# A third seven-product pair per gate and up unit, with two of its weight sums made by accumulating DMAs

## The chip, the cores and the metric

The kernel runs on one core of a Trainium2 chip. A time is the device time of one execution in microseconds (us). The kernel before takes 2226.62 us (median of 3 runs, 2225.67 to 2226.89). Profiles come from one execution of their own.

A core has engines that each work through their own list of instructions in order: TensorE (PE in the profile; PEld is its weight load) multiplies matrices into PSUM, eight banks of 512 floats per partition; VectorE (DVE), ScalarE (ACT) and GpSimd (POOL) work on elements; SyncE (SP) issues DMAs. An engine waits for another by semaphores, and what stands behind a waiting instruction in its list waits with it.

## The reference

One decoder layer in float32 on 256 tokens with 16 learned meta tokens ahead of them, model width 2048. Three blocks follow each other, each with a residual: a gated feed-forward, a mixer (differential attention and a short convolution, merged by gates), and a second gated feed-forward, then a last normalisation.

```python
def swiglu_ffn(h, w_gu, w_down):
    gate, up = jnp.split(h @ w_gu, 2, axis=-1)
    return (jax.nn.silu(gate) * up) @ w_down

h = rms_norm(s, norm_ffn2[layer])
s = s + 0.5 * swiglu_ffn(h, ffn2_w_gu[layer], ffn2_w_down[layer])
s = rms_norm(s, norm_final)
return s[:, N_META:]
```

The feed-forward width is 5632, so `w_gu` is 2048 x 11264: gate columns, then up columns. The change lies in the product with `w_gu` in the second feed-forward, where only the 256 real tokens are left.

## The kernel before

**Products in three matmuls.** Every float32 operand is split into a rounded high part and the remainder. For weights `parts` does it: ScalarE casts a tile into `wh`, VectorE subtracts it and writes `wl`. A product is then three matmuls: high by high, low by high, high by low. `wh` and `wl` have three buffers each (`W_BUFS`), so the splits run at most three tiles ahead of TensorE.

**The mixed unit.** In the second feed-forward the columns are taken in 11 groups of 512 gate and 512 up columns. Group 0 goes through a plain routine (`linear_tok`); the other ten each go through `gate_up_mix`, which calls `linear_mix`. Such a unit sums over 2048 input rows in 8 pairs of 128-row chunks. For one pair there are two token halves, two chunks and two column sets (gate and up), so a pair is a 2 x 2 by 2 x 2 block product. `KINDS` says for each of the 8 pairs how it is done:

- D (direct): eight block products. The weights come in two tiles of 1024 columns, each split and used in four products.
- S: a Strassen-like form with seven block products. It needs sums of the activation blocks, made once in `Mixed.pair` and kept in `sp`, and sums of the weight blocks, made anew in every unit. The weights come in four tiles: one of 512 columns (one product) and three of 1024 (two products each). The last two are sums and lie in `tt`: with w11, w12 the gate and up columns of the first chunk and w21, w22 those of the second, `tt` holds w11 + w12 (0), w12 + w22 (1), w11 + w12 + w22 (2) and that plus w21 (3). VectorE makes them by four additions (lines L507 to L510).

The products go to eight PSUM sums, "1" to "7" and "x"; `done` evicts each when its last product is in. The gating (L546 to L548: a sigmoid on ScalarE and two products on VectorE) follows from `flush`, called when the next unit's first pair has been used, and `back` transposes the gated result two tiles at a time for the down projection.

**Order of the work.** The program emits, for each tile, the split first and the tile's products two tiles later (`AHEAD` = 2, `step`). The framework's scheduler then fixes each engine's order when the kernel is built: by its own estimate of when things are ready it gives each engine the earliest emitted instruction that is ready, and gives buffers out as they come free. On the chip that order stands, and semaphores hold an instruction until its inputs are really there.

**Loads.** Weights come from memory through SP's queue into the buffers tagged `st`, 8 KB per partition each, of which there are four (`ST_BUFS`). In `linear_mix` a pair takes one buffer and two DMAs of 512 KB; an S pair takes a second buffer of the same tag for `tt`, without a DMA. A load stands in SP's queue until its buffer is free.

**Thirds.** The 11 groups go in three runs (4, 4 and 3 groups), each followed by two passes of the down projection (`linear_tok`, lines L318 to L320). So three of the ten mixed units come first after something else (group 1 after group 0, groups 4 and 8 after a down projection); the other seven follow another mixed unit. GpSimd's queue holds loads of small constants at the start and, in the last third, two loads of the last normalisation's gains (`gfin`).

Of the kernel before, what the change touches and what calls it, by code (L numbers as in the profile page):

```python
# [12 lines left out]
ALU = mybir.AluOpType  # L13
# [10 lines left out]
GW = GC * P  # L24
# [5 lines left out]
LAM_INIT = 0.8 - 0.6 * math.exp(-0.3 * 0)  # L30
KB = 2
W_BUFS = 3
ST_BUFS = 4
LB = 2
N_ACT = 24
EVICT_AT = 1
WARM = 6
HOLD = 3
LATER_AT = (4, 6)
KINDS = "DDDSDDDS"  # L40
AHEAD = 2


# [1 line left out]
def decoder_layer(ctx: ExitStack, tc: tile.TileContext, t, out):  # L45
    nc = tc.nc
# [7 lines left out]
    def bank(name):  # L54
        return psum.tile([P, 512], F32, tag="acc", name=name)
# [33 lines left out]
    def load_gain(g0, src):  # L89
# [5 lines left out]
        out=vrows[G_CONV:G_SUB, :], in_=t["conv_w"][0].rearrange("k (c p) -> (k c) p", p=P)  # L95
# [3 lines left out]
    for i, n in enumerate(("lambda_q1", "lambda_k1", "lambda_q2", "lambda_k2")):  # L99
# [7 lines left out]
        out=mask[:, T - P :],  # L107
        in_=mask[:, T - P :],
# [126 lines left out]
    def step(use):  # L235

        ahead.append(use)
        drain(AHEAD)
# [5 lines left out]
    def linear(act, chunks, w, k0, c0, t0, t1, name, evict, before=None, side_at=(5, 9, 13)):  # L244
# [7 lines left out]
        for b in range(0, len(chunks), kb):  # L252
# [5 lines left out]
            if b % nl == 0:  # L258
                st = wpool.tile([P, LB * kb, GW], F32, tag="st", bufs=ST_BUFS, name="st")
                ml = min(nl, len(chunks) - b)  # L260
# [40 lines left out]
    def flush():  # L301
        while pending:
            pending.pop(0)()

    def linear_tok(ops, chunks, k0, name, evict, side_at=(5, 9, 13), hold=0, after=None):
# [46 lines left out]
        for b, c in enumerate(chunks):  # L352
            if b % 2 == 0:
                st = wpool.tile([P, 2, 2, GW], F32, tag="st", bufs=ST_BUFS, name="st")
                r0 = (k0 + c) * P
# [9 lines left out]
    def parts(src, n=2):  # L365

        wh = wpool.tile([P, 2, GW], F32R, tag="wh", name="wh")[:, :n, :]
        wl = wpool.tile([P, 2, GW], F32R, tag="wl", name="wl")[:, :n, :]
        nc.scalar.copy(out=wh, in_=src)  # L369
        nc.vector.tensor_sub(wl, src, wh.bitcast(F32))  # L370
        return wh, wl
# [49 lines left out]
    class Mixed:  # L421
# [6 lines left out]
        def pair(self, p, f):  # L428
# [4 lines left out]
            nc.vector.tensor_sub(tl[:, :, 1, :], f, tl[:, :, 0, :].bitcast(F32))  # L433
            if KINDS[p] == "S":
                a11, a12, a21, a22 = (f[:, c, i * P : (i + 1) * P] for i in range(2) for c in range(2))
# [13 lines left out]
    def linear_mix(a, w, cols, name, done):  # L449

        nd, ns = KINDS.count("D"), KINDS.count("S")
        left = {k: 2 * nd * (k in "234x") + ns * (k != "x") for k in "1234567x"}
        ps = {}

        def product(k, left_op, wh, wl):
            first = k not in ps
            if first:
                ps[k] = bank(name + k)
            left[k] -= 1
            hi, lo = left_op
            nc.tensor.matmul(ps[k], hi, wh, start=first, stop=False)  # L467
            nc.tensor.matmul(ps[k], lo, wh, start=False, stop=False)  # L468
            nc.tensor.matmul(ps[k], hi, wl, start=False, stop=left[k] == 0)  # L469
            if left[k] == 0:  # L470
                done(k, ps[k])

        def use(p, n, products):

            for k, left_op, wh, wl in products:
                product(k, left_op, wh, wl)
            if p == len(KINDS) - 1 and n in (1, 2) and later:
                later.pop(0)()
            if n == (1 if KINDS[p] == "D" else 3):
                if p == 0:  # L480
                    flush()
                if side:
                    side.pop(0)()

        for p, kind in enumerate(KINDS):
            st = wpool.tile([P, 2, 2, GW], F32, tag="st", bufs=ST_BUFS, name="st")
            rows = w[2 * p * P : (2 * p + 2) * P, :].rearrange("(c p) f -> p c f", p=P)
            for q in range(2):
                nc.sync.dma_start(out=st[:, :, q, :], in_=rows[:, :, cols[q] : cols[q] + GW])
            (a11, a21), (a12, a22) = ([a.block(2 * p + c, i) for i in range(2)] for c in range(2))  # L490
            if kind == "D":
                tiles = [
                    (st[:, c], (("2", a1, 0), ("3", a1, 1), ("4", a2, 0), ("x", a2, 1)))
                    for c, (a1, a2) in enumerate(((a11, a21), (a12, a22)))
                ]
            else:
                s1, s2, s3, s4 = a.sums[p]
                tt = wpool.tile([P, 4, GW], F32, tag="st", bufs=ST_BUFS, name="tt")
                tiles = [
                    (st[:, 1, 1:2, :], (("3", s4, 0),)),  # L500
                    (st[:, :, 0, :], (("1", a11, 0), ("2", a12, 1))),
                    (tt[:, 2:4, :], (("6", s2, 0), ("4", a22, 1))),
                    (tt[:, 0:2, :], (("5", s1, 0), ("7", s3, 1))),
                ]
            for n, (src, products) in enumerate(tiles):
                if kind == "S" and n == 2:
                    nc.vector.tensor_add(tt[:, 0, :], st[:, 0, 0, :], st[:, 0, 1, :])  # L507
                    nc.vector.tensor_add(tt[:, 2, :], tt[:, 0, :], st[:, 1, 1, :])
                    nc.vector.tensor_add(tt[:, 3, :], tt[:, 2, :], st[:, 1, 0, :])
                    nc.vector.tensor_add(tt[:, 1, :], st[:, 0, 1, :], st[:, 1, 1, :])  # L510
                wh, wl = parts(src, src.shape[1])
                products = [(k, left_op, wh[:, j, :], wl[:, j, :]) for k, left_op, j in products]
                step(lambda p=p, n=n, products=products: use(p, n, products))

    def gate_up_mix(a, w_gu, g, m, gi):
# [3 lines left out]
        def done(k, ps):  # L519
# [21 lines left out]
            elif k == "7":  # L541
# [10 lines left out]
                pending.append(gated)  # L552

        linear_mix(a, w_gu, (g * GW, F + g * GW), "pg", done)

    def back(act, g, mt, k):
# [358 lines left out]
    for half in thirds:  # L915
# [10 lines left out]
        if final:  # L926
            for q in range(2):
                nc.gpsimd.dma_start(
                    out=gfin[q],
                    in_=t["norm_final"][q * W2 : (q + 1) * W2].rearrange("(o d) -> o d", o=1).to_broadcast([P, W2]),  # L930
# [47 lines left out]
```

## Time and profile before

| | |
|---|---|
| median of 3 runs | 2226.62 us |
| profiled execution, its own time | 2225.46 us |
| its span, first to last instruction | 2223.7 us |
| TensorE busy | 2205.9 us, 13608 matmuls |
| VectorE busy | 1376.3 us |
| ScalarE busy | 998.2 us |
| granted TensorE clock, mean | 0.998 |
| bytes moved by DMA | 401.95 MB, of it 1.21 MB on GpSimd's queue |

In the groups of a profile a row gives line, engine, operation, what is written and read, shapes and count; then busy time in us and the mean of one in ns; then the engine's idle time just before and what ended it. A row of the waits says which instruction waited for which, the total in us, how often, and the longest. A row of the order of time begins with the start from the span's begin and the length, both in us, and ends in brackets with the idle time before it. A matmul's length is longer than the distance to the next one, since matmuls overlap. "L507" is line 507 of the kernel before.

### The profile page before, as it was taken

To read this page: it belongs to the slowest core of one execution; us is meant where nothing else is said; L and a number is where in the kernel's file an instruction comes from. 1 tells how busy PE (TensorE), PEld (TensorE's weight loads), DVE (VectorE), ACT (ScalarE), POOL (GpSimd) and SP (SyncE) were. 2 spreads that over 40 slices of the span, in tenths; PEclk is the share of its full clock that TensorE was granted. 3 is DMA by queue.
4 is the path that set the end of the run, shared out by engine and by line. 5 is a ranking of instruction groups with operands and counts; after the bars stand their busy time and mean duration, and the time that the engine had idled before them with its cause. 6 is when DMAs were issued, how large, how long until landed. Compare 5 with 4: busy or idle time off the path is not lost.

```text
span 2223.7 us, 33100 instructions
## 1 busy us (share of the span) xinstructions
PE 2205.9 (99%) x13608; PEld 1989.5 (89%) x13608; DVE 1376.3 (62%) x1792; ACT 998.2 (45%) x1244; POOL 6.4 (0%) x17
## 2 busy tenths in 40 slices
PE   9999999999999999999999999999999999999998
PEld 8999999999999999898988888888888888888886
DVE  7555554455555565667765554668776578846875
ACT  6444343334434443444444444455454445534544
POOL 0000000000000000000000000000000000000000
PEclk9999999999999999999999999999999999999999
DMA  7555455555555455444555555555566555665563
GB/s 233 176 180 176 171 172 178 181 171 171 176 180 175 171 171 186 156 142 144 170 189 189 190 189 189 177 184 172 188 200 200 187 190 189 208 211 182 178 225 113
DMA packets 192023, 401.95 MB, mean 181 GB/s; under 512 B 8676, under 2 KB 8736, under 8 KB 191872
## 3 DMA queue, kind: packets, MB, share of 16 engines
q1 hardware_dynamic: 191232, 398.49, 53.0%
q8 instruction: 106, 1.74, 0.3%
q0 software_dynamic: 544, 1.21, 0.2%
q14 instruction: 45, 0.37, 0.0%
q10 hardware_dynamic: 96, 0.14, 0.0%
HBM read 397.71 MB, written 2.10 MB: 180 GB/s over the span
## 4 chain that ended last, share of the span: by engine, by line
PE 97%; DVE 1%; ACT 1%; DMA 0%; issue 0%; ACTq 0%; DVEq 0%
PE pg L467 5%; PE pg L469 5%; PE pg L468 5%; PE pg L282 4%; PE pg L280 4%; PE pd L282 4%; PE pu L282 4%; PE pu L280 4%; PE pg L281 4%; PE pd L280 4%; PE pd L281 4%; PE pu L281 4%; PE pd L320 4%; PE pd L318 4%; PE pd L319 4%; PE o L278 3%
## 5 line engine op out<-in xcount | busy, mean ns | idle before, releaser
L271 DVE TENSOR_TENSOR wl<-st,wh 128x1024 fp32r<-128x1024 f32 x392 | 478.5, 1223 | 442.4 <-ACT wh L270 442.1
L270 ACT CAST wh<-st 128x1024 fp32r<-128x1024 f32 x392 | 411.4, 1050 | 613.9 <-PE pd L281 146.9
L370 DVE TENSOR_TENSOR wl<-st,wh 128x1024 fp32r<-128x1024 f32 (+1 forms) x360 | 426.9, 1192 | 280.0 <-ACT wh L369 279.1
L369 ACT CAST wh<-st 128x1024 fp32r<-128x1024 f32 (+1 forms) x360 | 368.3, 1030 | 472.3 <-PE pgx L468 154.9
L280 PE MATMUL pg<-h,wh 128*128 128x272 f32 x704 | 203.3, 290 | 2.0 <-ACT wh L270 2.0
L280 PE MATMUL pu<-h,wh 128*128 128x272 f32 x704 | 203.3, 289 | 0.0
L282 PE MATMUL pu<-h,wl 128*128 128x272 f32 x704 | 203.0, 288 | 0.0
L282 PE MATMUL pd<-m,wl 128*128 128x272 f32 x704 | 203.0, 288 | 0.0
L280 PE MATMUL pd<-m,wh 128*128 128x272 f32 x704 | 202.9, 288 | 0.0
L281 PE MATMUL pd<-m,wh 128*128 128x272 f32 x704 | 202.4, 288 | 0.0
L281 PE MATMUL pu<-h,wh 128*128 128x272 f32 x704 | 202.4, 288 | 0.0
L281 PE MATMUL pg<-h,wh 128*128 128x272 f32 x704 | 202.4, 288 | 0.0
L282 PE MATMUL pg<-h,wl 128*128 128x272 f32 x704 | 201.1, 290 | 0.0
L467 PE MATMUL pg<-wh,hn 128*128 128x512 f32 x420 | 163.6, 390 | 0.0
L468 PE MATMUL pg<-wh,hn 128*128 128x512 f32 x420 | 163.5, 389 | 0.0
L469 PE MATMUL pg<-wl,hn 128*128 128x512 f32 x420 | 160.3, 391 | 0.0
L318 PE MATMUL pd<-wh,m 128*128 128x512 f32 x352 | 137.6, 391 | 0.0
L319 PE MATMUL pd<-wh,m 128*128 128x512 f32 x352 | 137.0, 389 | 0.0
L320 PE MATMUL pd<-wl,m 128*128 128x512 f32 x352 | 135.9, 390 | 0.0
L280 PEld LDWEIGHTS pg<-h,wh 128*128 128x128 f32 x704 | 132.9, 189 | 2.3 <-ACT wh L270 2.3
L281 PEld LDWEIGHTS pg<-h,wh 128*128 128x128 f32 x704 | 133.3, 189 | 0.0
L281 PEld LDWEIGHTS pu<-h,wh 128*128 128x128 f32 x704 | 132.7, 189 | 0.0
(279 smaller groups left out, 4536.4 us busy)
## 6 DMA issues: line engine op xcount, KB each, us to landing
st<-in_ffn_w_gu_dram SPq DMA_DIRECT2D x184, 512.0 KB, 4.3
st<-in_ffn_w_down_dram SPq DMA_DIRECT2D x88, 1024.0 KB, 5.1
st<-in_ffn_w_gu_dram SPq DMA_DIRECT2D x84, 1024.0 KB, 4.8
st<-in_w_in_dram SPq DMA_DIRECT2D x48, 1024.0 KB, 5.1
st<-in_w_gate_dram SPq DMA_DIRECT2D x64, 512.0 KB, 4.3
st<-in_w_branch_dram SPq DMA_DIRECT2D x32, 512.0 KB, 4.5
st<-in_w_out_dram SPq DMA_DIRECT2D x16, 1024.0 KB, 5.0
xin<-in_x_dram SPq DMA_DIRECT2D x8, 256.0 KB, 7.3
```

What stands on the lines that cost most here:

```text
L270: nc.scalar.copy(out=wh[:, :m, :], in_=sw)
L271: nc.vector.tensor_sub(wl[:, :m, :], sw, wh[:, :m, :].bitcast(F32))
L280: nc.tensor.matmul(a, wh[:, i, f], act.part(c, 0, t0, t1), start=first, stop=False)
L281: nc.tensor.matmul(a, wh[:, i, f], act.part(c, 1, t0, t1), start=False, stop=False)
L282: nc.tensor.matmul(a, wl[:, i, f], act.part(c, 0, t0, t1), start=False, stop=last)
L318: nc.tensor.matmul(ps, hi, wh[:, q, :], start=first, stop=False)
L319: nc.tensor.matmul(ps, lo, wh[:, q, :], start=False, stop=False)
L369: nc.scalar.copy(out=wh, in_=src)
L370: nc.vector.tensor_sub(wl, src, wh.bitcast(F32))
L467: nc.tensor.matmul(ps[k], hi, wh, start=first, stop=False)
L468: nc.tensor.matmul(ps[k], lo, wh, start=False, stop=False)
L469: nc.tensor.matmul(ps[k], hi, wl, start=False, stop=left[k] == 0)
```

## The change

`KINDS` becomes "DDSDDSDS": three S pairs (places 2, 5 and 7, counted from 0) where there were two (places 3 and 7). For an S pair, w12 is no longer loaded into `st`. Instead `tt`[0] is loaded with w11 and `tt`[1] with w22 by SP, and GpSimd's queue issues, for each, a DMA that adds w12 to what lies there. The additions L507 and L510 go; those that build `tt`[2] and `tt`[3] stay. A fifth buffer of the tag `st` comes in, and the memory set aside for GpSimd's DMA descriptors is set to 4096 bytes per partition.

```diff
-ST_BUFS = 4
+ST_BUFS = 5
...
-KINDS = "DDDSDDDS"
+KINDS = "DDSDDSDS"
...
             for q in range(2):
-                nc.sync.dma_start(out=st[:, :, q, :], in_=rows[:, :, cols[q] : cols[q] + GW])
+                c = q if kind == "S" else 0
+                nc.sync.dma_start(out=st[:, c:, q, :], in_=rows[:, c:, cols[q] : cols[q] + GW])
...
                 tt = wpool.tile([P, 4, GW], F32, tag="st", bufs=ST_BUFS, name="tt")
+                for q in range(2):
+                    nc.sync.dma_start(out=tt[:, q, :], in_=rows[:, q, cols[q] : cols[q] + GW])
+                    nc.gpsimd.dma_start(out=tt[:, q, :], in_=rows[:, 0, cols[1] : cols[1] + GW], accum_op=ALU.add)
...
                 if kind == "S" and n == 2:
-                    nc.vector.tensor_add(tt[:, 0, :], st[:, 0, 0, :], st[:, 0, 1, :])
                     nc.vector.tensor_add(tt[:, 2, :], tt[:, 0, :], st[:, 1, 1, :])
                     nc.vector.tensor_add(tt[:, 3, :], tt[:, 2, :], st[:, 1, 0, :])
-                    nc.vector.tensor_add(tt[:, 1, :], st[:, 0, 1, :], st[:, 1, 1, :])
...
-    nc = _bacc.Bacc("TRN2", target_bir_lowering=False, num_devices=1)
+    nc = _bacc.Bacc("TRN2", target_bir_lowering=False, num_devices=1, dynamic_dma_scratch_size=4096)
```

## The prediction

> **What bounds the kernel now.** I read the page first, then the groups of the second feed-forward (1500 us to the end), the waits, and the order of time on TensorE and VectorE around one seven-product pair.
>
> From the page:
>
> ```profile
> span 2223.7 us, 33100 instructions
> PE 2205.9 (99%) x13608; PEld 1989.5 (89%) x13608; DVE 1376.3 (62%) x1792; ACT 998.2 (45%) x1244; POOL 6.4 (0%) x17
> ...
> PE 97%; DVE 1%; ACT 1%; DMA 0%; issue 0%; ACTq 0%; DVEq 0%
> ```
>
> TensorE carries the chain; only fewer products, or fewer stalls of TensorE, can shorten it. The change touches only the ten mixed units, so their rows count. TensorE in the order of time, just where such a unit goes from the second to the third tile of its first S pair:
>
> ```profile
> 1857.62 0.39 PE L468 MATMUL pg<-wh,hn 128*128 128x512 f32 x1
> ...
> 1858.53 0.39 PE L469 MATMUL pg<-wl,hn 128*128 128x512 f32 x1
> 1859.34 0.50 PE L467 MATMUL pg<-wh,sp 128*128 128x512 f32 x1 [0.42 <-ACT wh L369]
> ```
>
> Two readings. The 0.39 us is a length; the pitch, over four of them (three left out), is (1858.53 - 1857.62) / 4 = 0.2275 us, and that is what a matmul costs. And here the pitch breaks: 1859.34 - 1858.53 = 0.81 us, a stall of 0.58 us. The waits tell how often, and what is late:
>
> ```profile
> PE pg L467 <- ACT wh L369: 2.1, 5, 0.4
> ...
> ACT wh L369 <- DVE tt L509: 21.3, 7, 3.2
> ...
> DVE tt L507 <- DMA st<-in_ffn_w_gu_dram: 6.2, 3, 2.8
> ```
>
> In 7 of 10 units the cast of the summed weights waits for the last sum (L509) on VectorE; in 5 of them TensorE stands still for it, in 2 it only just does not. The other 3 units, first after a down projection, show none of it. The third row is used below.
>
> **The change, part by part.**
>
> *Products.* One more S pair in place of a D pair: 7 products instead of 8, 3 matmuls each. 3 x 0.2275 = 0.68 us a unit, 10 units: -6.8 us. This lies on TensorE, on the path.
>
> *Where the first S pair stands.* It moves from place 3 to place 2, so TensorE comes to its third tile 24 x 0.2275 = 5.46 us sooner. VectorE before that point, in the unit above:
>
> ```profile
> 1847.64 1.22 DVE L370 TENSOR_TENSOR wl<-st,wh 128x1024 fp32r<-128x1024 f32 x1
> 1848.78 1.21 DVE L547 TENSOR_TENSOR cgate<-cgate,u2x 128x1024 f32<-128x1024 f32 x1
> 1849.91 1.22 DVE L370 TENSOR_TENSOR wl<-st,wh 128x1024 fp32r<-128x1024 f32 x1
> 1851.05 1.21 DVE L548 TENSOR_TENSOR cup<-cup,cgate 128x1024 f32<-128x1024 f32 x1
> 1852.18 1.81 DVE L370 TENSOR_TENSOR wl<-st,wh 128x1024 fp32r<-128x1024 f32 x2
> 1853.92 0.68 DVE L507 TENSOR_TENSOR tt<-st 128x512 f32<-128x512 f32 x1
> 1855.10 1.23 DVE L370 TENSOR_TENSOR wl<-st,wh 128x1024 fp32r<-128x1024 f32 x1 [0.49 <-ACT wh L369]
> 1856.24 0.68 DVE L508 TENSOR_TENSOR tt<-tt,st 128x512 f32<-128x512 f32 x1
> 1856.84 0.69 DVE L510 TENSOR_TENSOR tt<-st 128x512 f32<-128x512 f32 x1
> 1857.44 0.68 DVE L509 TENSOR_TENSOR tt<-tt,st 128x512 f32<-128x512 f32 x1
> ```
>
> VectorE works without a gap until 1854.60: it is still evicting the unit before (L547, L548) and splitting. The change takes two splits of the D pair at place 2 (1.13 us each from start to start) and L507 and L510 out of this stretch, 3.5 us against the 5.46 us that TensorE comes sooner. In this clock: L547 at 1848.78, the small split at 1849.91 (+0.60), L548 at 1850.51 (+1.13), the second split at 1851.64 (+1.14), the first remaining sum at 1852.78 (+0.72, since the next reads it; pitch below), the second at 1853.50, done 1854.18. TensorE starts 1859.34 - 1858.12 = 1.22 us after the last sum: 1855.40. It could at 1858.53 + 0.23 - 5.46 = 1853.30. Stall 2.1 us, where it was 0.58: +1.5 us, 5 units. The milder kind:
>
> ```profile
> 1804.94 1.21 DVE L547 TENSOR_TENSOR cgate<-cgate,u2x 128x1024 f32<-128x1024 f32 x1
> ...
> 1812.72 0.68 DVE L508 TENSOR_TENSOR tt<-tt,st 128x512 f32<-128x512 f32 x1
> 1813.44 0.69 DVE L509 TENSOR_TENSOR tt<-tt,st 128x512 f32<-128x512 f32 x1
> ...
> 1815.06 0.39 PE L469 MATMUL pg<-wl,hn 128*128 128x512 f32 x1
> 1815.35 0.50 PE L467 MATMUL pg<-wh,sp 128*128 128x512 f32 x1
> ```
>
> Same steps from 1804.94: TensorE at 1811.56, could at 1809.83: 1.7 us where it was 0.06, +1.65 us, 2 units. The first units of a third have room, a row from each side of it:
>
> ```profile
> 1769.21 1.23 DVE L370 TENSOR_TENSOR wl<-st,wh 128x1024 fp32r<-128x1024 f32 x1 [2.46 <-ACT wh L369]
> ```
>
> VectorE idles 2.46 us before one split there; 0 for 3 units. Sum: 5 x 1.5 + 2 x 1.65 = +10.8 us. Ends: 0 (the gating products fall behind the sums) and +15.
>
> *The two sums by DMA.* Each S pair now needs, before its sums: the slot of tt free, a 256 KB load on SP's queue, its landing, then an accumulating DMA of 256 KB on POOL's queue, which waits for that landing. No accumulating DMA is in the trace. Nearest rows:
>
> ```profile
> DMA to landing us min/median/max: 3.4/4.3/6.4
> ...
> st<-in_ffn_w_gu_dram SPq DMA_DIRECT2D x184, 512.0 KB, 4.3
> ...
> gfin<-in_norm_final_dram POOLq DMA_DIRECT2D x2, 512.0 KB, 8.4
> ...
> vrows<-in_norm_mix_dram POOLq DMA_DIRECT2D x1, 8.0 KB, 4.9
> ```
>
> The load: 3.4 us or a little less, being half as large. The accumulation: from 4.9 us (8 KB on POOL's queue) to twice 8.4 = 16.8 us; I take 8, near the row of 512 KB, since it reads 256 KB of weights and the 256 KB that it adds to. Chain: 11.4 us, bounds 8 to 20. SP's next loads stand behind the load's wait for the slot, the pair's second accumulation behind the first. [...]
>
> How long it may take: five buffers of that tag, 11 takings a unit. The tt at place 5 takes the slot of the st at place 2, free when the second sum there is done (1854.18). TensorE reaches the third tile at place 5 after 2 S tiles, two D pairs and 2 S tiles (69 matmuls), 15.7 us after 1855.40; less 1.22 and two sums, the accumulated tile may come at 1868.5: 14.3 us. The tt at place 7 takes the slot of the D pair at place 4: from that pair's second tile TensorE has 66 matmuls to go, 15.0 us, less the same 2.6: 12.4 us and the lead that the split had over TensorE. That at place 2 takes the slot of the st at place 7 of the unit before: 69 matmuls again, 13.1 us and that lead. So 11.4 us would do, if VectorE took the sums when they are needed. But its order is fixed when the kernel is built, by the scheduler's own estimate of landings, and that is too early already for one plain load:
>
> ```profile
> 1561.49 0.69 DVE L507 TENSOR_TENSOR tt<-st 128x512 f32<-128x512 f32 x1 [2.77 <-DMA st<-in_ffn_w_gu_dram]
> ```
>
> L507 stood at the head of VectorE's queue for 2.77 us until a load landed (6.2 us in 3 units), with the splits of later tiles behind it; TensorE had weights in hand and lost nothing. For a load and an accumulation in a row the error is more: 2.1 us (6.2 / 3) for the load, and up to 8.4 - 4.3 = 4.1 us if POOL's DMAs are planned like SP's; together 2 to 6 us. What waits behind the sums: splits, casts (their wh buffers), then TensorE. 2.8 us were free in a stretch of D tiles; at place 7 the wait falls among the tiles of place 5, where a tile lasts 0.68 to 1.37 us of TensorE and covers less. Per S pair at places 5 and 7: 0 to 3.4 us (6.2 - 2.8), I take 1.0: 20 pairs, +20 us, ends 0 and +68. At place 2 the VectorE backlog hides it, 0.
>
> *The rest.* VectorE per unit: two splits fewer, four more (one small), 8 sums become 6: 35.4 of 44.0 us busy as before.
>
> ```profile
> 1858.60:1902.60 44.00, 43.58 (x196) 35.47 (x194) 35.43 (x40) 22.29 (x26) 0.00 (x0) 1.00 0.56 192
> ```
>
> DMA share 0.56 at 8.4 MB a unit; 10.8 MB after (9.2 by SP, 1.6 by POOL), 12.3 with the second read: 0.72 to 0.82, not a bound, 0. POOL's 60 issues lie on an engine that is busy 6.4 us in all, and the only others in this stage, the two of gfin, are through before the last third's units begin: 0. The fifth buffer lets loads run earlier everywhere, but no row of TensorE waits for one: 0. The third set of activation sums (four small sums, a cast and a split, once) hides beside the first unit, where TensorE shows no wait: 0. The smaller descriptor scratch: 0.
>
> **Sum** against the profiled execution (span 2223.7, its own time 2225.46): -6.8 + 10.8 + 20 = +24 us, 2249.5; that execution stands 1.2 us below the median of 2226.62, so 2250 of the median.
>
> **The rivals.**
>
> 1. *The chain is in time and the sums stand late enough.* Only the backlog at place 2 is left: -6.8 + 10.8 = +4.0, 2230.6. For it: the 14.3 us against 11.4. Against it: the L507 row. This stands on the 0.2% line (4.5 us, about what a measurement of this kernel can tell from no change).
> 2. *Faster: neither wait is there.* The scheduler puts the gating behind the sums at place 2, and the chain is in time. With L548 alone behind (1.13 us) the stalls are 1.0 and 0.6, +3 us: 2222.8. With L547 too they are gone, and the old ones (5 x 0.58 + 2 x 0.06 = 3 us) with them: 2216.8. Middle 2219.8. It decides once VectorE has over 1 us less ahead of the sums. For it: VectorE is busy only 35.4 of 44.0 us. Against it: the gating stands earlier in the program than place 2.
> 3. *The accumulation is slow.* At 16.8 us the chain is 20.2, 5.9 us over the 14.3 of place 5 in ten units, 59, and as much as 41 more at place 7, of which the stall at place 5 covers a part: +4 and 60 to 100, 2290 to 2330.
>
> **How the numbers follow.** Forecast 0.45, rival 1 0.18, rival 2 0.20, rival 3 0.17. Faster by over 0.2%: rival 2, 0.20. Within: half of rival 1, 0.09. Slower: 0.71. Range: from the middle of rival 2, 2219, to 2292 (forecast with most of +68), which leaves out most of rival 3; the forecast's own range is 2231 to 2290.
>
> **What would show it.** Matmuls 13608 - 30 = 13578; POOL 60 more DMA rows. In the waits, VectorE's first sum waiting for a DMA of tt, some 20 to 30 times, and TensorE or ScalarE waiting for VectorE's splits after it. At place 2 the stall near 2 us in 7 units. The landing of the accumulation near 8 us; under 5 points to rivals 1 and 2, over 12 to rival 3. The prediction is wrong if the sums wait for no DMA, or if VectorE's order at place 2 has the sums ahead of the gating.

## The result and the profile after

The changed kernel takes 2318.51 us (median of 4 runs, 2314.31 to 2324.7) against 2226.57 us: a ratio of 1.0416, 95% interval 1.0392 to 1.0440. It is slower by 92 us, above the predicted 2250 and above the range.

The page of the profile after (profiled execution 2317.39 us):

```profile
span 2315.5 us, 33444 instructions
...
PE 2230.2 (96%) x13578; PEld 2001.4 (86%) x13578; DVE 1387.0 (60%) x1797; ACT 1015.0 (44%) x1265; POOL 58.4 (3%) x77
...
q0 software_dynamic: 9184, 16.94, 4.1%
...
PE 85%; DVE 6%; DMA 5%; issue 2%; ACT 1%; DVEq 0%; ACTq 0%; SPq 0%; POOLq 0%
```

The 30 matmuls are gone. But the chain that ended last, 97% TensorE before, now runs for 6% over VectorE and for 5% over DMA. The waits say which DMA (line numbers of the changed kernel: L502 issues the accumulating DMAs, L511 and L512 are the two sums):

```profile
DVE tt L511 <- DMA tt<-in_ffn_w_gu_dram: 92.8, 23, 8.1
...
PE pg L469 <- DVE wl L370: 57.6, 12, 7.6
...
ACT wh L369 <- DVE tt L512: 32.2, 7, 4.7
...
PE pg L467 <- ACT wh L369: 11.8, 7, 1.7
```

The first sum waits for an accumulation 23 times in 30, for 92.8 us. TensorE waits in two places: 57.6 us for the low parts of weights (L370), for which its waits before have no row, and 11.8 us for casts behind the sums (2.1 us before). The order of time shows how the first comes about. This is the end of one unit, from the last buffer's release on; SPq is SyncE's queue:

```profile
1663.40 1.19 SPq L501 DMA_DIRECT2D tt<-in_ffn_w_gu_dram  x2
...
1667.92 1.73 POOL L502 DMA_DIRECT2D tt<-in_ffn_w_gu_dram  x2 [11.06 <-DVE wl L370]
...
1668.26 2.00 ACT L369 CAST wh<-tt 128x1024 fp32r<-128x1024 f32 x2 [1.67 <-PE pgx L468]
...
1670.56 0.39 PE L468 MATMUL pg<-wh,sp 128*128 128x512 f32 x1
1675.97 0.69 DVE L511 TENSOR_TENSOR tt<-tt,st 128x512 f32<-128x512 f32 x1 [8.12 <-DMA tt<-in_ffn_w_gu_dram]
1676.70 0.69 DVE L512 TENSOR_TENSOR tt<-tt,st 128x512 f32<-128x512 f32 x1
1677.31 2.35 DVE L370 TENSOR_TENSOR wl<-tt,wh 128x1024 fp32r<-128x1024 f32 x2
1678.58 0.80 PE L469 MATMUL pg<-wl,sp 128*128 128x512 f32 x1 [7.64 <-DVE wl L370]
1679.18 0.63 PE L467 MATMUL pg<-wh,hn 128*128 128x512 f32 x1
1679.60 0.63 PE L468 MATMUL pg<-wh,hn 128*128 128x512 f32 x1
```

Read it from L511. This is the sum for place 7, and it reached the head of VectorE's queue at 1667.85 (1675.97 - 8.12), just as its accumulation was being issued. So VectorE stood for the whole flight. Behind L511 and L512 in the queue are the two splits of `tt` (L370), and these belong to place 5: ScalarE had cast those tiles from 1668.26 on. TensorE does the two matmuls that need only the high part, up to 1670.56, and then has nothing until 1678.58. The tile that L511 prepared was not wanted before all of place 5 and the D pair at place 6 were through.

There is a second loss. After the stall matmuls start every 0.42 us (1679.18, 1679.60), not 0.2275. The same stretch by engine, with the granted clock as the last column but two, and 490 us of the stage:

```profile
1678.50:1690.00 11.50, 11.42 (x38) 9.21 (x39) 5.44 (x6) 3.53 (x4) 0.00 (x0) 0.73 0.58 187
...
1500.00:1990.00 490.00, 440.70 (x1862) 355.74 (x1861) 322.75 (x373) 220.11 (x245) 36.37 (x42) 0.94 0.66 198
```

The same 490 us in the kernel before:

```profile
1500.00:1990.00 490.00, 488.31 (x2178) 400.83 (x2178) 356.94 (x412) 237.65 (x262) 0.91 (x2) 1.00 0.57 192
```

The granted clock was 0.73 there and 0.94 in the stage, where before it was 1.00. From 1490 us on the records show it at half for 82 us, in fifteen pieces of 3.4, 6.8 or 10.2 us, each beginning during a stall or within 1.7 us of its end. Two more pieces are not counted, 3.4 us at the start of the kernel and 8.4 us at its end, which the kernel before has too (3.4 and 8.1). The fifteen pieces begin whole multiples of 3.413 us apart. Stalls of 1.9 us were enough for one: all five of them here, and two of five in the run with late sums.

The account: over the matmuls from 1490 us to the end I added what each start-to-start distance has above the pitch. Before: about 7.5 us. After: about 106 us. The difference, 98 to 99 by the pitch that one takes, less the 6.8 us of products saved, is some 92, and the spans differ by 91.8. Of the 106, 57.7 us are ten stalls at place 7's sums, one a unit (2.3 to 7.8 us each), 13.0 us are seven stalls at place 2, 1.9 us lie at place 5, some 4 us are the small unevenness that was there before, and the rest, about 29 us, is matmuls at half clock. Three of the ten stalls at place 7 are short, 2.3 to 2.9 us: the accumulation there was issued 1.2 to 1.4 us before the sum came up, and landed 4.0 to 4.4 us after its issue, against 6.1 to 8.2 in the other seven. Why it landed sooner is open.

### The profile page after: what moved, and what is told of

Its sections match the earlier page's. It is cut to its first block, busy times and chain, and to the rows that moved or that the text cites. A ratio compares the mean times of both kernels' runs of the same rounds, so it can differ in the third digit from the quotient of the medians.

```text
span 2315.5 us, 33444 instructions
## 1 busy us (share of the span) xinstructions
PE 2230.2 (96%) x13578; PEld 2001.4 (86%) x13578; DVE 1387.0 (60%) x1797; ACT 1015.0 (44%) x1265; POOL 58.4 (3%) x77
## 3 DMA queue, kind: packets, MB, share of 16 engines
q0 software_dynamic: 9184, 16.94, 4.1%
## 4 chain that ended last, share of the span: by engine, by line
PE 85%; DVE 6%; DMA 5%; issue 2%; ACT 1%; DVEq 0%; ACTq 0%; SPq 0%; POOLq 0%
DMA tt<-in_ffn_w_gu_dram 5%; PE pg L282 4%; PE pg L280 4%; PE pd L282 4%; PE pu L282 4%; PE pu L280 4%; PE pd L280 4%; PE pg L281 4%; PE pd L281 4%; PE pu L281 4%; PE pd L320 3%; PE pd L318 3%; PE pd L319 3%; PE pg L469 3%; PE o L278 3%; PE g L320 3%
## 5 line engine op out<-in xcount | busy, mean ns | idle before, releaser
L370 DVE TENSOR_TENSOR wl<-st,wh 128x1024 fp32r<-128x1024 f32 (+1 forms) x360 | 422.4, 1178 | 277.9 <-ACT wh L369 276.9
L467 PE MATMUL pg<-wh,hn 128*128 128x512 f32 x390 | 156.2, 401 | 0.0
L468 PE MATMUL pg<-wh,hn 128*128 128x512 f32 x390 | 155.6, 399 | 0.0
L469 PE MATMUL pg<-wl,hn 128*128 128x512 f32 x390 | 152.5, 404 | 1.6 <-DVE wl L370 1.5
```

## The experiments

Two theories stood after this. **Place in the queue:** the accumulations are fast enough, but the scheduler put the place-7 sums ahead of place 5's splits, where everything behind them waits. **Landing:** the accumulations come too late whatever the order, so that TensorE waits for them anyway.

### The sums later in VectorE's queue

The two sums are held behind the split of the first tile of their own S pair (places 2, 5 and 7).

```diff
-                    nc.vector.tensor_add(tt[:, 2, :], tt[:, 0, :], st[:, 1, 1, :])
-                    nc.vector.tensor_add(tt[:, 3, :], tt[:, 2, :], st[:, 1, 0, :])
+                    with tc.issue_after(split_ins[-2]):
+                        nc.vector.tensor_add(tt[:, 2, :], tt[:, 0, :], st[:, 1, 1, :])
+                        nc.vector.tensor_add(tt[:, 3, :], tt[:, 2, :], st[:, 1, 0, :])
```

> The changed kernel with its two remaining sums held, in VectorE's order, behind the split of the first tile of their own S pair; nothing else differs. Theory Q (place in the queue): the loss is that the sums of place 7 stand in VectorE's order ahead of the splits of place 5's summed tiles and wait there, up to 8.1 us, for an accumulation that TensorE does not need until a pair and a half later. Then the stalls at place 7 (57.7 us in ten units) and the half-clock stretches after them go; left are the 6.8 us gained in products and about 10 us lost at place 2: 2228 to 2240 us. Rival L (late chain): the load and the accumulation in a row are simply too slow for their slot; then the stall only moves to the cast of the summed tile and the time stays over 2280 us.

Measured: 2233.51 us, ratio 1.0033 [1.0020, 1.0046]. 85 us of the 92 are back. Its waits (L471 is the low-part matmul, L514 and L515 the sums):

```profile
PE pg L469 <- ACT wh L371: 11.8, 7, 1.8
```

```profile
DVE tt L514 <- DMA tt<-in_ffn_w_gu_dram: 3.8, 4, 1.3
...
ACT wh L371 <- DVE tt L515: 32.2, 7, 4.7
```

The 57.6 us are gone entirely, and the sum waits for an accumulation 4 times instead of 23, 1.3 us at most. Bytes, transfers and buffers are the same, so the landing theory falls: taken where they are needed, the accumulations are there. What is left is the seven stalls at place 2, and VectorE's order in front of one shows why:

```profile
1636.01 1.22 DVE L553 TENSOR_TENSOR cup<-cup,cgate 128x1024 f32<-128x1024 f32 x1
1637.15 1.22 DVE L372 TENSOR_TENSOR wl<-st,wh 128x1024 fp32r<-128x1024 f32 x1
1638.29 0.68 DVE L514 TENSOR_TENSOR tt<-tt,st 128x512 f32<-128x512 f32 x1
1639.00 0.69 DVE L515 TENSOR_TENSOR tt<-tt,st 128x512 f32<-128x512 f32 x1
```

No gap, and the gating of the unit before (L553) just ahead. The stall behind it was 1.9 us, the predicted kind.

### Late at place 7 alone

As above, but held only where `p == 7`; at places 2 and 5 the sums are issued as in the changed kernel.

> The changed kernel with the two sums held behind the split of the S pair's first tile at place 7 alone; at places 2 and 5 they are issued as in the changed kernel. Theory (the loss is the place-7 sums standing ahead of the split of place 5's summed tiles: 57.7 us of TensorE's stalls, and the half clock after them): what is left is the 13.0 us of the seven stalls at place 2, the 1.9 us at place 5 and the half clock of some 7 us behind these, so 2233.5 to 2242. Rival (every place where VectorE waits takes its share: 25 us of waits at place 5): the waits at place 5 now reach TensorE, and the time is 2250 to 2275.

Measured: 2236.83 us, ratio 1.0048 [1.0031, 1.0065].

```profile
PE pg L469 <- ACT wh L371: 11.8, 7, 1.7
...
PE pg L471 <- DVE wl L372: 0.7, 2, 0.5
```

```profile
DVE tt L514 <- DMA tt<-in_ffn_w_gu_dram: 32.1, 17, 3.8
```

So the loss is place 7's. VectorE still stands 32.1 us for accumulations, up to 3.8 us at a time, some 25 us of it at place 5, and TensorE feels 0.7 us of it. At place 5 the tiles ahead are those of two D pairs; at place 7 they are those of an S pair and one D pair.

### Accumulating DMAs, but S pairs at 3 and 7 as before

```diff
-KINDS = "DDSDDSDS"
+KINDS = "DDDSDDDS"
```

> The accumulating DMAs and five buffers of the changed kernel, but two S pairs at places 3 and 7 as before. Theory Q: what counts is what stands behind the waiting sums. With three D pairs between the S pairs the sums of place 7 wait among tiles of D pairs, where 2.8 us of waiting cost nothing before: a loss of 0 to 25 us, 2220 to 2252 us. Rival L: two thirds of the loss of the changed kernel, near 2290 us.

Measured: 2224.89 us, ratio 0.9995 [0.9986, 1.0005].

```profile
DVE tt L511 <- DMA tt<-in_ffn_w_gu_dram: 36.8, 11, 4.2
...
```

VectorE waits 36.8 us for accumulations, and the time does not move. The sums are not held late here. Where D pairs lie ahead, waits of up to 4.2 us at the head of VectorE's queue cost TensorE 0.8 us in all, and replacing two sums by two DMAs gains nothing that the runs could tell either.

### All four sums on VectorE

S pairs at 2, 5 and 7, five buffers, no accumulating DMA: the kernel before with `KINDS = "DDSDDSDS"`.

> Three S pairs at places 2, 5 and 7 and five buffers as in the changed kernel, but all four sums on VectorE and no accumulating DMA. Theory Q: nothing waits for a landing at the head of VectorE's queue; -6.8 us of products, and at place 2 a backlog larger by two sums (1.2 us) than in the changed kernel, 7 units: 2232 to 2245 us. Rival P (the third S pair itself, through VectorE's load, makes the loss): over 2280 us.

Measured: 2248.09 us, ratio 1.0097 [1.0082, 1.0113], a little over what I expected.

```profile
PE pg L467 <- ACT wh L369: 15.6, 7, 2.2
```

With two more sums ahead of it the stall at place 2 is 2.40 us seven times (from start to start; the row counts idle time alone, up to 2.2), and the half clock lasts 17 us in the stage against 7 with late sums. The two DMAs a pair are worth 15 us at these places, when the sums stand late, and cost 70 when they do not.

### The fifth buffer and the smaller scratch alone

```diff
-ST_BUFS = 4
+ST_BUFS = 5
...
-    nc = _bacc.Bacc("TRN2", target_bir_lowering=False, num_devices=1)
+    nc = _bacc.Bacc("TRN2", target_bir_lowering=False, num_devices=1, dynamic_dma_scratch_size=4096)
```

> The kernel before with the fifth buffer and the smaller descriptor memory, nothing else. All theories: within 3 us of the kernel before, 2224 to 2230 us. If it is slower by more than 5 us, a part of the loss belongs to the buffer count or the descriptor memory.

Measured: 2226.53 us, ratio 1.0003 [0.9993, 1.0012]. Nothing, as costed.

### A plain copy in place of the accumulation

The copy overwrites what SyncE's load brought, so this kernel leaves w11 and w22 out of the sums.

```diff
-                    nc.gpsimd.dma_start(out=tt[:, q, :], in_=rows[:, 0, cols[1] : cols[1] + GW], accum_op=ALU.add)
+                    nc.gpsimd.dma_start(out=tt[:, q, :], in_=rows[:, 0, cols[1] : cols[1] + GW])
```

> The changed kernel with the add taken out of GpSimd's 60 transfers: each now writes w12 over the 256 KB that SyncE's transfer brought, instead of adding to it, so the two sums lack w11 and w22 and the output is another one. Bytes, queues, issue order and VectorE's work stay. If it is the add (a read of the target and an addition on the way) that makes these transfers last a median of 6.7 us, they fall to about the 2.9 us of SyncE's transfers of 256 KB in the same kernel, the waits of L511 for them (92.8 us, 23) shrink to under 40 us, and the time lies at 2250 to 2280. If it is the way the transfer is issued (GpSimd's queue, beside SyncE's loads), the landing stays at 5.5 to 8 us and the time at 2300 to 2325.

Measured: 2268.14 us (a single run). The DMA rows, of the changed kernel first and then of this run:

```profile
tt<-in_ffn_w_gu_dram SPq DMA_DIRECT2D x60, 256.0 KB, 2.9
tt<-in_ffn_w_gu_dram POOLq DMA_DIRECT2D x60, 256.0 KB, 6.7
```

```profile
q0 software_dynamic: 5344, 16.94, 2.4%
...
tt<-in_ffn_w_gu_dram SPq DMA_DIRECT2D x60, 256.0 KB, 3.0
tt<-in_ffn_w_gu_dram POOLq DMA_DIRECT2D x60, 256.0 KB, 3.6
```

It is the add that costs: on the same queue, with the same bytes and every engine's instructions in the same order, a transfer lands in a median of 3.6 us as a copy (I had expected about 2.9) and in 6.7 us as an accumulation, and the queue carries 5344 packets against 9184. The accumulation takes 1.9 times as long (6.7 by 3.6). Half the landing takes away about half the loss, since VectorE waits out what is left of the flight:

```profile
DVE tt L511 <- DMA tt<-in_ffn_w_gu_dram: 37.4, 19, 6.3
```

### The gating later

With the late sums, `flush` (the gating of the unit before) is called after place 3 instead of place 0.

```diff
-                if p == 0:
+                if p == 3:
                     flush()
```

> S pairs at 2, 5 and 7, accumulating DMAs, sums behind the first split, and the gating of the unit before (ACT's sigmoid, VectorE's two products) moved from the end of place 0 to the end of place 3. If the gating ahead of place 2 is the backlog, the 7 stalls of 1.7 to 1.9 us there go to under 0.6 us each and the half clock with them: 2233.5 - 10 to 13 = 2219 to 2224. If the backlog is that of the evictions, or moves on to place 5, the stalls stay at 1.5 us and more, at 2 or at 5, and the time is 2230 to 2240.

Measured: 2224.34 us, ratio 0.9992 [0.9983, 1.0002]: the time is at the edge of what I expected of the gating as the backlog, but the stalls are not under the 0.6 us that I named.

```profile
PE pg L469 <- ACT wh L371: 6.4, 7, 0.9
```

```profile
1633.35 0.69 DVE L514 TENSOR_TENSOR tt<-tt,st 128x512 f32<-128x512 f32 x1
1633.95 1.22 DVE L552 TENSOR_TENSOR cgate<-cgate,u2x 128x1024 f32<-128x1024 f32 x1
1635.09 0.69 DVE L515 TENSOR_TENSOR tt<-tt,st 128x512 f32<-128x512 f32 x1
1635.69 1.22 DVE L553 TENSOR_TENSOR cup<-cup,cgate 128x1024 f32<-128x1024 f32 x1
```

The stalls fall from 1.9 to 1.07 us, and there is no half clock left. One gating product (L553) is now behind the sums. The other (L552) the scheduler slips in between them, and it takes 1.14 us from start to start, about what remains.

### S pairs at 3, 5 and 7

The late sums with `KINDS = "DDDSDSDS"`; `flush` stays after place 0.

> Three seven-product pairs by the accumulating DMAs, at places 3, 5 and 7 instead of 2, 5 and 7, with the two sums held behind the split of the S pair's first tile (as in the run at 2233.51). Theory (all that is left of the loss there is the backlog of the gating at place 2: 7 stalls of 1.7 to 1.9 us, 13.0 in all, and the half clock behind them): at place 3 one more D pair lies ahead, as in the kernel before, where the stalls there are 0.58 and 0.06 us, so the 6.8 us of saved products come through: 2226.1 - 6.8 = 2219, range 2216 to 2223. Rival (the S pairs themselves are too dense for VectorE, wherever the first stands): stalls of 0.5 us and more come up at places 5 and 7, and the time is 2226 to 2235.

Measured: 2220.94 us, ratio 0.9974 [0.9964, 0.9985]. This is faster than the kernel before. In its waits no row of TensorE for the S pairs is left:

```profile
PE mt_ps L566 <- ACT cup L532: 1.8, 2, 1.3
PE pd L320 <- DVE wl L372: 1.2, 2, 0.6
```

The same places with all four sums on VectorE (five buffers, no accumulating DMA):

> As the run before this one, S pairs at places 3, 5 and 7, but all four sums on VectorE and no accumulating DMA. With the S pairs at 2, 5 and 7 that was 2248.09 with 7 stalls of 2.40 us at place 2. If that loss is the backlog at place 2 and the half clock behind it, 2219 to 2230 here; if two more sums per S pair (about 1.3 us of VectorE each) are too many in themselves, stalls at 5 and 7 and 2235 to 2250. If the accumulating DMAs are worth anything once the sums stand at the right place, this is slower than the run with them by 2 us or more.

Measured: 2223.11 us, ratio 0.9987 [0.9978, 0.9996].

```profile
PE pg L467 <- ACT wh L369: 2.1, 5, 0.4
...
PE pg L469 <- DVE wl L370: 1.2, 3, 0.7
```

So of the 5.0 us gained (2225.91 beside these runs), 2.8 come with the third S pair alone, the first one staying at place 3, and 2.2 more with the DMAs and the late sums together, which is about the least that I had named for them to be worth anything.

### Four S pairs

Late sums, `KINDS = "DSDSDSDS"`, `flush` after place 2.

> Four seven-product pairs, at places 1, 3, 5 and 7, by accumulating DMAs, sums behind the first split, and the gating moved from the end of place 0 to the end of place 2. Against the run at places 3, 5 and 7 (2220.94) it saves another 6.8 us of products. If the accumulations stay in time with an S pair at every second place and VectorE keeps up, 2213 to 2218. If VectorE or the DMA queues are full (one D pair between two S pairs all along), stalls of 1 us and more per unit at the odd places, and 2222 to 2250.

Measured: 2252.03 us, ratio 1.0116 [1.0101, 1.0131], a little over the 2250 at which I had ended the rival.

```profile
PE pg L469 <- ACT wh L371: 19.3, 7, 2.8
PE pg L471 <- DVE wl L372: 4.8, 7, 0.8
```

```profile
1586.34 1.22 DVE L372 TENSOR_TENSOR wl<-st,wh 128x1024 fp32r<-128x1024 f32 x1
1587.47 0.69 DVE L514 TENSOR_TENSOR tt<-tt,st 128x512 f32<-128x512 f32 x1
1588.08 1.22 DVE L552 TENSOR_TENSOR cgate<-cgate,u2x 128x1024 f32<-128x1024 f32 x1
1589.21 0.69 DVE L515 TENSOR_TENSOR tt<-tt,st 128x512 f32<-128x512 f32 x1
```

My rival named stalls "at the odd places"; they are all at place 1, two in each of seven units (2.9 us, and 0.6 to 1.0 us), and none is at 3, 5 or 7. Place 1 follows at once on the evictions of the unit before, and one gating product (L552) again stands between the sums. So the S pairs at 3, 5 and 7 are not too dense; the first one, as I read it, stands too near the unit's start. That a fourth pair elsewhere would pay was not tried.

## Why the prediction was wrong

*Products, -6.8:* right. 13578 matmuls, and with the stalls at the S pairs gone most of it shows (5.0 us, with the S pairs at 3, 5 and 7).

*Place 2, +10.8:* right in mechanism and size. Predicted stalls of 2.1 and 1.7 us in 5 and 2 units, 13.9 us in all where 3.0 was; measured 1.7 to 1.9 us in 7 units, 13.0. Moving the gating (1.07 us left) and moving the pair one place on (none left) both confirm the backlog as the cause.

*The sums by DMA, +20:* this is the step that failed, at the words "Per S pair at places 5 and 7: 0 to 3.4 us (6.2 - 2.8), I take 1.0". The mechanism was the one named there: L511 at the head of VectorE's queue, splits behind it. Even the place was named: at place 7 "the wait falls among the tiles of place 5" where less covers it. But I then gave both places one mean, chosen between two ends and not worked out. Measured, place 5 costs 0.2 us a pair (1.9 in ten) and place 7 costs 5.8 (57.7 in ten), beyond the 3.4 that I allowed a pair. Two numbers behind those ends were off for place 7. The wait was put at 2 to 6 us, as the scheduler's error; it was 2.6 to 8.1 us, since the sum came up within 1.7 us of the issue of its accumulation. And 2.8 us, seen among D tiles, was taken as free; at place 7 nearly nothing was (a wait of 8.12 made a gap of 7.64). At place 5 somewhat more was free than I thought: waits of up to 3.4 us cost nothing, one of 3.5 cost 0.5 us and one of 4.5 cost 1.4.

*The landing:* 8 us taken, 6.7 measured. No view shows the second read that the 8 us and the 12.3 MB a unit counted: GpSimd's queue carries 16.94 MB with the add and without it. And a chain of 11.4 us would indeed have done, as rival 1 said: the run with late sums is that rival, 2233.5 against its 2230.6. Rival 3 has the time right (2290 to 2330) and the cause wrong: no accumulation of the changed kernel took more than 9.2 us.

*What stood in no term:* the clock, put at nothing without a reason. The end at +68 prices stalls at their length only, and the half clock behind them added about 29 us more. So 60 us at places 5 and 7 lay inside the ends of the term, and the total still went past 2292. That the half clock follows from the stalls is read from the records (the last section says which stalls); no run took it away by itself.

*The rest:* the fifth buffer and the scratch at 0 were right. At place 2 the sums waited for DMAs only in the three units first in a third, about 2 us each, and TensorE lost nothing by it, as predicted. The DMA share, predicted at 0.72 to 0.82 in a unit, is diluted by the stalls in the changed kernel (0.66), and 0.73 to 0.76 over the stage in the runs with three S pairs and late sums.

## What to carry to other kernels

An instruction that waits for a long chain of DMAs costs what stands behind it in its engine's queue, not what it does itself (here two sums of 0.69 us each kept TensorE waiting for 5.8 us a pair at place 7 and 0.2 us at place 5): find its place in that order, ask what the next instructions feed, and price each place by itself, for a mean over a covered and an uncovered place fits neither. Where a scheduler fixes the order by its own estimates, tie such an instruction to the point where its result is needed; here one such line was worth 85 us, and without it the change was a loss. And price a TensorE stall above its length once it nears 2 us: here the clock was at half behind thirteen of twenty stalls of 1.9 us, and behind none of eight of 1.7 us.

## What the hardware showed that I had not expected

- **Short stalls lower the clock.** Stalls are counted from start to start, less the pitch. Seven of 1.07 us: no half clock. Eight of 1.7 us, in four runs: none. Twenty of 1.9 us, in the same four: a piece of 3.4 us behind thirteen, among them five of five in the changed kernel and two of five with late sums. Seven of 2.40 us: 17.1 us of half clock, after five. Seven of 2.9 us with another of 0.6 to 1.0 us just ahead: 20.5 us, after six. Seven of 6.6 to 7.8 us: a piece of 6.8 or 10.2 us begun within each.
- **Where a stall falls decides it.** In each run the pieces begin whole multiples of 3.413 us apart, so the time can be divided into stretches of 3.413 us on that grid. The profiles of six runs (the changed kernel, late sums, late at place 7 alone, all sums on VectorE, plain copy, four pairs) hold 53 stalls of 1.1 to 4.3 us. The 30 that lay for 1.91 us or more in one stretch had the clock halved in the next; the 23 that had at most 1.79 us in any one stretch had not. So by these traces a stall of 1.7 us costs its length alone, and one of 1.9 us costs clock if it happens to fall inside one stretch.
- **The accumulation's price is on the DMA's side.** 6.7 us against 3.6 for the copy. Whether it slows its neighbours is not shown: SyncE's 512 KB loads of the same stage land in a median of 4.3 us before, 4.7 beside the plain copies, and 5.1 and 5.6 in two runs with late sums, but in 4.5 in the changed kernel, which has the same accumulations.
